# Two token tiles of gMLP's v in place of two gate tiles in the last attention blocks, and an eighth pair of gate columns

## The chip, the cores and the metric

The kernel runs on one core of one Trainium2 chip. The metric is the device time of one execution in microseconds (us). Five engines work side by side, each on a queue of its own and in the order of that queue: TensorE (PE; its weight loads are shown as PEld), VectorE (DVE), ScalarE (ACT), GpSimd (POOL) and SyncE (SP), which here issues nearly all DMAs.

## The reference

One decoder layer works on 576 tokens, 512 of a prompt and 64 of eight running requests, with a model width of 1024:

```python
h   = x @ w_in          # columns: gMLP u | gMLP v | q | k | attention v | gate_A | gate_B
u   = gelu(h_u);  v = LayerNorm(gelu(h_v))
y_A = u * (tril(W_s) @ v_chunk + b_s)        # inside chunks of 128 tokens
y_B = sliding_window_attention(q, k, v_attn) # 16 heads, 4 key heads, sinks, relative bias
m   = (sigmoid(gate_A) * (y_A @ w_pa) + sigmoid(gate_B) * (y_B @ w_pb)) @ w_o
x   = LN1(alpha * x + m);  x = LN2(alpha * x + (silu(x @ w_gate) * (x @ w_up)) @ w_down)
```

gate_A and gate_B have 1024 columns each, so 16 column tiles of 128. u has eight column tiles. v is computed the other way round, with tokens on the partitions: five token tiles (numbers 0 to 3 of 128 prompt tokens each, number 4 of the 64 sample tokens), in two halves of 512 columns.

## The kernel before

**Precision.** Each f32 operand is split in two: `hi`, a rounded copy that ACT makes (line 117), and `lo`, the rest, which DVE makes (line 118). A product is hi*hi + hi*lo + lo*hi, so three matmuls. The weights come from HBM as units of 128x1024 f32 (512 KB, tiles `raw`, three buffers). A unit's `hi` and `lo` have four buffers each, and are written over when PE has read them.

**A plain column tile** (`fm`, called by `column_tile`) takes 8 chunks of the contraction, 3 matmuls each, on two halves of 288 tokens: 48 matmuls 288 wide. **A pair of column tiles** (`pair`) computes two of them together by a Winograd-like scheme with 7 products in place of 8, each of 4 chunks with 3 matmuls: 84 matmuls 288 wide for two tiles. Its products are named B11, T1, T2, B22, B21, T3 and T4. Their weight sides are made by `weight_group` out of two units: DVE and POOL subtract blocks ("sums", step 3; the tiles `t` and `raw`, line 180), and four splits (`ghi`, `glo`) follow in steps 1, 3, 2 and 4, T2 and T3 being parts of `t`. The input's sides S1, S2 and S4 (`XS1`, `XS2`, `XS4`) are made once by `input_sum` out of a second load of x (`xr`, four chunks, two loads of 288 KB each), and S3 (`X<-s`) by `input_sum3`, which writes over a part of `X` that the last v products still read.

**The stages around the change, in order.** (1) Sixteen attention blocks (4 key heads by 4 token blocks). Block i turns its probabilities (`pT`), selects with POOL's masks (`pc`, `pt`), and multiplies by the values (`po`); between these PE runs a fill, which the list `FILLS` names. The last two fills were the gate tiles g0 and g1 (`psg`). ACT's exponentials for the sample tokens (`samS`, line 703) run beside block 14's fill. (2) The first half of v (`acc_v0`): four weight units, and for each of them all five token tiles; the sample's attention values (`pso`) and three of the four `input_sum`s lie in it. (3) The second half of v (`acc_v1`): tiles 0, 1 and 2 one after the other, then 3 and 4 together, with gelu on ACT, and statistics and normalisation (lines 337 to 355, the reciprocal root on POOL as `lnr`) on DVE. (4) The pairs of gates (`merge`, tiles `xg`, `yg`, `zg`), seven of them, where the weights of pair i+1 are prepared beside pair i. A pair's last product, T4, runs inside the next pair. Two `spatial_gate`s (`sgu`) lie in each of pairs 2 to 5, and the key outputs (`pskout`) in pair 1. (5) The output side (`pspa`, `xp`, `acc_o`, `ffn`, `xf`, `d`), which the change does not touch.

Up to stage 3 a scheduler places the instructions of each engine from priorities and its own costs; `issue_after` holds an instruction behind another one. Inside `manual_schedule` (the pairs) the written order counts. SP's queue is one line too: a load of `xr` that waits for its buffer holds the weight loads behind it.

Of the kernel before, what the change touches and what calls it, by code (L numbers as in the profile page):

```python
# [70 lines left out]
FILLS = [tuple(x) for x in "q3 u0 k1 q4 q5 u1 q6 q7 u2 u3 u4 u5 u6 u7 g0 g1".split()]  # L71
# [8 lines left out]
class Builder:  # L80
# [678 lines left out]
    def projections_and_attention(self):  # L759
# [6 lines left out]
        self.kt, self.qs, self.u, self.T = [], {}, [], []  # L766
# [25 lines left out]
        for i, (g, n) in enumerate(blocks):  # L792
# [18 lines left out]
            fill = self.column_tile(*fills[i], ahead=1 + before_last)  # L811
# [18 lines left out]

    def column_tile(self, kind, c, ahead=1):

        ps = self.PS(f"ps{kind}{c}")
        u = self.unit(KC, ahead=ahead)
        self.fm(ps, u, self.xact, ks=range(7))
        yield
        self.fm(ps, u, self.xact, ks=range(7, KC))
        yield
        if kind == "k":
            self.evac_k(ps, c)  # L840
        elif kind == "q":
            self.evac_q(ps, c)
        else:
            tiles = self.u if kind == "u" else self.T
            if c % 2 == 0:
                tiles.append(self.C([2, NT], F32, f"{kind}{c}"))
            self.copied = self.nc.scalar.copy(
                out=tiles[c // 2][:, c % 2].rearrange("p (b c) -> p b c", b=2), in_=ps[:, :, :HB])
# [27 lines left out]
    def gmlp(self):  # L876
# [26 lines left out]
        def tile(t, out, u, ks):  # L903
            for k in ks:
                wh, wl = u[k // 2]
                self.tm(out, (*self.xact(k), self.XS[:, k, :]), wh[:, k % 2], wl[:, k % 2], t, k == 0, k == KC - 1)

        def evacuate(t, acc, half):
# [3 lines left out]
            else:  # L912
# [4 lines left out]
                nc.scalar.activation(out=v[t][:NS, s], in_=low[:NS, :512], func=AF.Gelu_apprx_tanh)  # L917
# [4 lines left out]
        acc = self.accumulators("v0")  # L922
        for n in range(4):
            with self.tc.issue_after(self.copied.ins):
                u = {n: self.unit(2)}
            for t in range(NB + 1):
                tile(t, acc[t], u, (2 * n, 2 * n + 1))
            if n == 0:
                self.sample_rest()
            if n == 1:  # L930
                self.input_sums()
                for c in range(3):
                    self.input_sum(c)
                fourth = self.input_loads(3)
        for t in range(NB + 1):
            evacuate(t, acc[t], 0)
        with self.tc.issue_after(self.turned.ins):
            for t in self.u:
                nc.scalar.activation(out=t[:], in_=t[:], func=AF.Gelu_apprx_tanh)
        us = [self.unit(2, ahead=int(n < 3)) for n in range(4)]  # L940
        for t in range(3):
            acc = self.bank(f"acc_v1_{t}")
            tile(t, acc, us, range(KC))
            if t == 0:
                with self.tc.issue_after(self.last_split.ins):
                    self.input_sum(3, fourth)
# [72 lines left out]
    def merge(self):  # L1019
        nc = self.nc  # L1020
        for t in self.T:
            nc.scalar.activation(out=t[:], in_=t[:], func=AF.Sigmoid)
        left = self.left(self.X, (*self.XSums[:2], self.input_sum3(), self.XSums[2]))
        self.first_pair(self.low_added)
        T = [self.T[0][:, i] for i in range(2)]
        gB = []
# [7 lines left out]
        def gates(i, g, u, more):  # L1034
            def final(x):
                self.copied = nc.scalar.activation(out=g[:, HB:], in_=x, func=AF.Sigmoid)
                nc.scalar.activation(out=u[:], in_=u[:], func=AF.Sigmoid)

            first = lambda: nc.scalar.activation(out=g[:, :HB], in_=g[:, :HB], func=AF.Sigmoid)
            self.pair(f"g{i}", left, g, u, first, final, more)  # L1040
# [370 lines left out]
def _weights(w_in, w_pa, w_pb, w_o, w_gate, w_up, w_down):  # L1411
# [113 lines left out]
```

## Time and profile before

| | |
|---|---|
| runs | median 876.85 us (876.51, 876.85, 876.95) |
| the profiled execution | 876.51 us, its span 874.8 us |
| granted TensorE clock | 0.998 |
| instructions | 14728 |

The page gives each engine's busy time and the chain of work that ended last, which is followed back from the last instruction. The timeline of an engine has the start, the duration, the engine, the line, the operation, output and input and, in brackets, the idle time before it and what ended it. Where several instructions are merged, x2 stands behind them, and the time runs from the first start to the last end. Matmul durations overlap, so a matmul's pace is read from the distance of starts, or from rows of the chain, which don't overlap.

### The profile page before, as it was taken

How to read it: one execution, taken by the hardware profiler on the slowest of the kernel's cores; microseconds unless marked ns; L12 is line 12 of the kernel's file. 1: busy time of each engine (PE TensorE's matmuls, PEld its weight loads, DVE VectorE, ACT ScalarE, POOL GpSimd, SP SyncE). 2: the span in 40 equal slices, each digit the busy share in tenths (PEclk: the TensorE clock that was granted, in tenths of full speed). 3: DMA queues.
4: the chain of work that ended last, by engine and by line, in shares of the span. 5: the costliest groups of instructions: out<-in, count | busy, mean ns of one | idle time of the engine just before them, and what ended most of it. 6: DMA issues, size and time to landing. Idle time of an engine off the chain costs nothing.

```text
span 874.8 us, 14728 instructions
## 1 busy us (share of the span) xinstructions
PE 864.8 (99%) x5907; PEld 816.8 (93%) x5907; DVE 629.4 (72%) x933; ACT 405.5 (46%) x770; POOL 194.5 (22%) x206
## 2 busy tenths in 40 slices
PE   9999999999999999999999999999999999999996
PEld 7999999988899999999888999999999998888885
DVE  5878897657898888767778767777777789124237
ACT  6566566575464464333423544444444557111110
POOL 2013324253242203133203122222222210000003
PEclk9999999999999999999999999999999999999999
DMA  8422124255123134324640032222222335222202
GB/s 304 156 100 62 61 73 148 61 175 163 47 100 102 63 121 142 118 98 157 217 144 0 13 101 91 92 93 91 90 90 95 95 105 188 94 75 95 73 1 108
DMA packets 31168, 91.85 MB, mean 105 GB/s; under 512 B 3963, under 2 KB 9244, under 8 KB 31068
## 3 DMA queue, kind: packets, MB, share of 16 engines
q1 hardware_dynamic: 30764, 88.64, 30.9%
q10 hardware_dynamic: 336, 2.28, 0.7%
q8 instruction: 46, 0.75, 0.4%
q14 instruction: 22, 0.18, 0.1%
HBM read 86.77 MB, written 6.10 MB: 106 GB/s over the span
## 4 chain that ended last, share of the span: by engine, by line
PE 94%; DVE 3%; ACT 1%; DMA 0%; issue 0%; POOL 0%; DVEq 0%; SPq 0%; POOLq 0%; ACTq 0%
PE d L300 16%; PE xf L300 15%; PE zf L300 7%; PE acc_v L300 6%; PE acc_o L300 6%; PE pspa L300 6%; PE xg L300 5%; PE psu L300 5%; PE yf L300 4%; PE psq L300 4%; PE ffn L300 3%; PE xp L300 3%; PE zg L300 3%; PE psav L300 2%; PE psg L300 1%; PE zp L300 1%
## 5 line engine op out<-in xcount | busy, mean ns | idle before, releaser
L118 DVE TENSOR_TENSOR lo<-raw,hi 128x1024 fp32r<-128x1024 f32 x70 | 87.5, 1255 | 94.0 <-ACT hi L117 93.7
L118 DVE TENSOR_TENSOR glo<-raw,ghi 128x1024 fp32r<-128x1024 f32 (+1 forms) x93 | 100.5, 1087 | 53.6 <-ACT ghi L117 53.6
L300 PE MATMUL d<-hi,h 128*128 128x512 f32 (+1 forms) x440 | 128.0, 368 | 0.0
L117 ACT CAST hi<-raw 128x1024 fp32r<-128x1024 f32 x70 | 72.7, 1049 | 103.2 <-PE d L300 82.6
L117 ACT CAST ghi<-raw 128x1024 fp32r<-128x1024 f32 (+1 forms) x93 | 83.4, 900 | 58.7 <-DVE raw L180 56.9
L300 PEld LDWEIGHTS d<-hi,h 128*128 128x128 f32 x440 | 79.9, 189 | 13.8
L300 PE MATMUL d<-lo,h 128*128 128x512 f32 (+1 forms) x242 | 89.6, 370 | 0.0
L180 POOL TENSOR_TENSOR raw<-raw,t 128x512 f32<-128x512 f32 x31 | 41.0, 1323 | 193.3 <-DVE glo L118 164.1
L180 POOL TENSOR_TENSOR t<-raw,raw 128x512 f32<-128x512 f32 x31 | 43.0, 1387 | 111.9 <-DVE raw L180 111.9
L300 PE MATMUL xf<-x1T,ghi 128*128 128x288 f32 x320 | 64.9, 295 | 0.0
L118 DVE TENSOR_TENSOR glo<-t,ghi 128x1024 fp32r<-128x1024 f32 x31 | 63.0, 2032 | 1.9 <-ACT ghi L117 1.9
L300 PEld LDWEIGHTS d<-lo,h 128*128 128x128 f32 x242 | 45.6, 189 | 7.8
L300 PEld LDWEIGHTS xf<-x1T,ghi 128*128 128x128 f32 x320 | 51.3, 188 | 0.3 <-DVE u L231 0.2
L330 POOL TENSOR_SCALAR lnr<-lnmv 128x1 f32<-128x1 f32 (+1 forms) x15 | 12.3, 818 | 169.8 <-DVE lnmv L348 166.5
L645 POOL TENSOR_SCALAR_AFFINE_SELECT pc<-pt 128x512 fp32r<-128x512 f32 x24 | 23.1, 963 | 110.8 <-ACT pt L117 102.7
L300 PE MATMUL xf<-x1T,glo 128*128 128x288 f32 x160 | 47.1, 294 | 0.0
L300 PE MATMUL acc_o<-hi,m 128*128 128x512 f32 x144 | 46.4, 391 | 0.0
L621 ACT ACTIVATE work<-work,att 128x128 f32<-128x128 f32 x64 | 25.0, 392 | 42.1 <-DVE att L618 37.5
L300 PE MATMUL pspa<-yA,hi 128*128 128x288 f32 x256 | 44.3, 294 | 0.0
L300 PE MATMUL psu<-X,hi 128*128 128x288 f32 x256 | 44.1, 294 | 0.0
L300 PE MATMUL acc_v<-hi,X 128*128 128x512 f32 x128 | 41.8, 391 | 0.0
L300 PE MATMUL psq<-X,hi 128*128 128x288 f32 x224 | 38.8, 294 | 0.3 <-DVE kt L513 0.3
(370 smaller groups left out, 2472.6 us busy)
## 6 DMA issues: line engine op xcount, KB each, us to landing
raw<-in_wall_dram SPq DMA_DIRECT2D x132, 512.0 KB
open<-in_open_dram SPq DMA_DIRECT2D x7, 416.0 KB
xr<-in_xT_dram SPq DMA_DIRECT2D x8, 288.0 KB
z<-in_xtok_dram SPq DMA_DIRECT2D x4, 512.0 KB
out_y_prompt_dram<-z SPq DMA_DIRECT2D x3, 512.0 KB
circ<-bout SPq DMA_DIRECT2D x1, 1024.0 KB
Bsel<-circ SPq DMA_DIRECT2D x2, 512.0 KB
kc<-in_kcT_dram SPq DMA_DIRECT2D x2, 512.0 KB
```

Source lines behind the costliest of these rows:

```text
L117: self.nc.scalar.copy(out=hi, in_=src)
L118: return self.nc.vector.tensor_tensor(out=lo, in0=src, in1=hi.bitcast(F32), op=ALU.subtract)
L180: sub = lambda e, out, x, y: e.tensor_tensor(out=out, in0=x, in1=y, op=ALU.subtract)
L300: self.last_mm = self.nc.tensor.matmul(out, l, r, start=start, stop=stop, **more)
L330: self.nc.gpsimd.tensor_scalar_add(r[:n], mv[:n, 1:2], EPS)
L621: nc.scalar.activation(out=pr[:, r], in_=sel[:, r], func=AF.Exp, bias=nm[:, r : r + 1], accum_out=rs[:, r : r + 1])
L645: self.selected = nc.gpsimd.affine_select(out=f(out[:, i]), in_=f(pt[:, i].bitcast(F32)), pattern=[[0, 4], [sign, P]], compare_op=cmp, fil ...
```

## The change

- `FILLS` ends with v0 and v1 in place of g0 and g1. The new `value_tile` computes token tiles 0 and 1 of v's first half there, and ACT copies the sums to `v0raw`; gelu and statistics follow after the attention. For these tiles all four weight units of v's first half are converted before the attention ends.
- The first half of v then has only tiles 2, 3 and 4. Its unit buffers are kept for it, and each unit of the second half is converted (`ahead=0`) when tiles 2 to 4 have used a unit of the first. The sample's values move behind the second unit, the `input_sum`s to one per unit, and the gelus of u behind tile 4's first gelu.
- g0 and g1 become pair 0 of eight. The gates' first sigmoid moves from the middle of a pair to its end, and `first_pair`, the first pair's weight split, is written ahead of `input_sum3`.

```diff
-FILLS = [tuple(x) for x in "q3 u0 k1 q4 q5 u1 q6 q7 u2 u3 u4 u5 u6 u7 g0 g1".split()]
+FILLS = [tuple(x) for x in "q3 u0 k1 q4 q5 u1 q6 q7 u2 u3 u4 u5 u6 u7 v0 v1".split()]
...
+    def value_tile(self, t):
+        ps = self.PS(f"psv{t}")
+        if t == 0:
+            self.v0w = [self.unit(2, ahead=int(n < 3)) for n in range(4)]
+            self.v0raw = self.C([2, 512], F32, "v0raw")
+        self.value_part(t, ps[:, 0], self.v0w, range(7))
+        yield
+        self.value_part(t, ps[:, 0], self.v0w, range(7, KC))
+        yield
+        self.copied = self.nc.scalar.copy(out=self.v0raw[:, t], in_=ps[:, 0])
...
-        acc = self.accumulators("v0")
+        acc = {t: self.bank(f"acc_v0_{t}") for t in (2, 3, NB)}
+        with self.tc.issue_after(self.turned.ins):
+            for t in range(2):
+                evacuate(t, self.v0raw[:, t], 0)
+        us = []
         for n in range(4):
-            with self.tc.issue_after(self.copied.ins):
-                u = {n: self.unit(2)}
-            for t in range(NB + 1):
-                tile(t, acc[t], u, (2 * n, 2 * n + 1))
+            for t in acc:
+                tile(t, acc[t], self.v0w, (2 * n, 2 * n + 1))
+            us.append(self.unit(2, ahead=0))
             if n == 0:
-                self.sample_rest()
-            if n == 1:
                 self.input_sums()
-                for c in range(3):
-                    self.input_sum(c)
-                fourth = self.input_loads(3)
+                chunk = self.input_loads(0)
+            else:
+                if n == 1:
+                    self.sample_rest()
+                self.input_sum(n - 1, chunk)
+                chunk = self.input_loads(n)
...
-        with self.tc.issue_after(self.turned.ins):
+        with self.tc.issue_after(self.gelu.ins):
             for t in self.u:
                 nc.scalar.activation(out=t[:], in_=t[:], func=AF.Gelu_apprx_tanh)
-        us = [self.unit(2, ahead=int(n < 3)) for n in range(4)]
...
-        for t in self.T:
-            nc.scalar.activation(out=t[:], in_=t[:], func=AF.Sigmoid)
+        self.first_pair(self.low_added)
         left = self.left(self.X, (*self.XSums[:2], self.input_sum3(), self.XSums[2]))
-        self.first_pair(self.low_added)
...
-                nc.scalar.activation(out=u[:], in_=u[:], func=AF.Sigmoid)
-
-            first = lambda: nc.scalar.activation(out=g[:, :HB], in_=g[:, :HB], func=AF.Sigmoid)
-            self.pair(f"g{i}", left, g, u, first, final, more)
+                for t in (g[:, :HB], u[:]):
+                    nc.scalar.activation(out=t, in_=t, func=AF.Sigmoid)
+
+            self.pair(f"g{i}", left, g, u, lambda: None, final, more)
...
-            for i in range(7):
+            for i in range(8):
```

Of the program's order, three places follow. Names carry a running number, which differs between the two programs.

**ACT at the end of the attention**, from the last exponential of the last block (line 623) on; `pt_2` and `pt_3` are the last two blocks' turned probabilities, `bot` the lower half of their values. Before:

```order
L623 ACTIVATE att<-att 128x4
L847 COPY u_2094<-psu_2096 128x576
L117 CAST pt_2_2157<-pT_2_2152 128x512
L658 COPY bot_1_2170<-po_1_2165 64x512
L703 ACTIVATE samS,satt<-samS,satt 128x136 x8
L705 ACTIVATE satt<-satt,misc 128x8
L117 CAST pt_3_2292<-pT_3_2287 128x512
L658 COPY bot_2_2305<-po_2_2300 64x512
L847 COPY g_2309<-psg_2226 128x576
L658 COPY bot_3_2359<-po_3_2354 64x512
L847 COPY g_2309<-psg_2311 128x576
```

Of the change:

```order
L623 ACTIVATE att<-att 128x4
L117 CAST hi_2241<-raw_2227 128x1024
L867 COPY u_2094<-psu_2096 128x576
L117 CAST pt_2_2157<-pT_2_2152 128x512
L658 COPY bot_1_2170<-po_1_2165 64x512
L703 ACTIVATE samS,satt<-samS,satt 128x136 x8
L705 ACTIVATE satt<-satt,misc 128x8
L117 CAST pt_3_2275<-pT_3_2270 128x512
L658 COPY bot_2_2288<-po_2_2283 64x512
L850 COPY v0raw<-psv_2226 128x512
L658 COPY bot_3_2320<-po_3_2315 64x512
L850 COPY v0raw<-psv_2293 128x512
```

One weight cast, that of v's fourth unit, has come ahead of block 14's turned probabilities; on DVE its `lo` stands at the same place. The copies of the fills are those of v instead of g.

**DVE ahead of the first pair of gates**, from the statistics of v's tile 2 on; `glo_0` is the low part of B11 and T1, `glo_2` of T3 and T2, `glo_4` of B22 and B21, `X<-s` are the four chunks of S3, `vlow` is tile 4's sum. Before:

```order
L337 BN_STATS lnst<-v_2416 128x6
L348 BN_AGGR lnmv<-lnst 128x2
L118 TENSOR_TENSOR X<-s_0_2553,X 128x288
L353 SCALAR_TENSOR_TENSOR v_2416<-v_2416,lnmv,lnvg 128x1024
L118 TENSOR_TENSOR X<-s_0_2553,X 128x288
L355 SCALAR_TENSOR_TENSOR v_2416<-v_2416,lnr,lnvb 128x1024
L118 TENSOR_TENSOR X<-s_1_2554,X 128x288 x2
L118 TENSOR_TENSOR glo_0_2886<-raw_2699,ghi_0_2885 128x1024
L118 TENSOR_TENSOR glo_2_2892<-t_2881,ghi_2_2891 128x1024
L915 TENSOR_TENSOR vlow_2863<-acc_v_4_2822,vlow_2863 64x512
L118 TENSOR_TENSOR glo_4_2896<-raw_2705,ghi_4_2895 128x1024
```

Of the change:

```order
L337 BN_STATS lnst<-v_2374 128x6
L348 BN_AGGR lnmv<-lnst 128x2
L118 TENSOR_TENSOR X<-s_0_2415,X 128x288
L353 SCALAR_TENSOR_TENSOR v_2374<-v_2374,lnmv,lnvg 128x1024
L118 TENSOR_TENSOR X<-s_0_2415,X 128x288
L355 SCALAR_TENSOR_TENSOR v_2374<-v_2374,lnr,lnvb 128x1024
L118 TENSOR_TENSOR glo_0_2767<-raw_2529,ghi_0_2766 128x1024
L118 TENSOR_TENSOR X<-s_1_2416,X 128x288
L118 TENSOR_TENSOR glo_2_2773<-t_2762,ghi_2_2772 128x1024
L118 TENSOR_TENSOR X<-s_1_2416,X 128x288
L930 TENSOR_TENSOR vlow_2753<-acc_v_4_2712,vlow_2753 64x512
L118 TENSOR_TENSOR glo_4_2777<-raw_2565,ghi_4_2776 128x1024
```

Two of S3's four chunks now stand behind `glo_0`. Further ahead on DVE, the last chunk of the input's sums stands between the two halves of tile 0's normalisation, as the scheduler put it, and on ACT the four gelus of u stand between tile 4's first gelu and tile 2's second.

**ACT from the end of pair 0 into pair 1** (pair 0's tile is `T_2902` before and `T_2791` now, pair 1's `T_3021` and `T_2909`; `ghi_2`, `ghi_4`, `ghi_0`, `ghi_6` are the splits for pair 1's B22 and B21, its T2 and T3, pair 2's B11 and T1, and pair 1's T4). Before:

```order
L252 COPY T_2902<-xg_2903 128x288
L1039 ACT_TABLE_LOAD
L1039 ACTIVATE T_2902<-T_2902 128x288
L117 CAST ghi_2_2999<-raw_2906 128x1024
L117 CAST ghi_4_3017<-t_2908 128x1024
L243 COPY T_3021<-xg_3022 128x288
L246 COPY T_3021<-zg_3024 128x288
L117 CAST ghi_0_3056<-raw_2950 128x1024
L1036 ACTIVATE T_2902<-xg_2903 128x288
L1037 ACTIVATE T_2902<-T_2902 128x576
L117 CAST ghi_6_3076<-raw_2906 128x512
L252 COPY T_3021<-xg_3022 128x288
```

Of the change:

```order
L252 COPY T_2791<-xg_2792 128x288
L117 CAST ghi_2_2887<-raw_2795 128x1024
L117 CAST ghi_4_2905<-t_2797 128x1024
L243 COPY T_2909<-xg_2910 128x288
L246 COPY T_2909<-zg_2912 128x288
L117 CAST ghi_0_2944<-raw_2839 128x1024
L1052 ACT_TABLE_LOAD
L1052 ACTIVATE T_2791<-xg_2792 128x288
L1054 ACTIVATE T_2791<-T_2791 128x288
L1054 ACTIVATE T_2791<-T_2791 128x576
L117 CAST ghi_6_2965<-raw_2795 128x512
L252 COPY T_2909<-xg_2910 128x288
```

The first sigmoid and the load of the sigmoid's table have left the place ahead of `ghi_2`, and stand ahead of `ghi_6`.

More of the change, by code (lines that the diff above doesn't have):

```diff
@@ L810, in projections_and_attention @@
             before_last = i + 2 == len(blocks)
-            fill = self.column_tile(*fills[i], ahead=1 + before_last)
+            if fills[i][0] == "v":
+                fill = self.value_tile(fills[i][1])
+            else:
+                fill = self.column_tile(*fills[i], ahead=1 + before_last)
             next(fill, None)
@@ L843, in column_tile @@
         else:
-            tiles = self.u if kind == "u" else self.T
             if c % 2 == 0:
-                tiles.append(self.C([2, NT], F32, f"{kind}{c}"))
-            self.copied = self.nc.scalar.copy(
-                out=tiles[c // 2][:, c % 2].rearrange("p (b c) -> p b c", b=2), in_=ps[:, :, :HB])
+                self.u.append(self.C([2, NT], F32, f"{kind}{c}"))
+            self.nc.scalar.copy(
+                out=self.u[c // 2][:, c % 2].rearrange("p (b c) -> p b c", b=2), in_=ps[:, :, :HB])
     def small_tables(self):
@@ L916, in evacuate @@
                     out=low[:NS, :512], in0=acc[:NS], in1=low[:NS, :512], op=ALU.add)
-                nc.scalar.activation(out=v[t][:NS, s], in_=low[:NS, :512], func=AF.Gelu_apprx_tanh)
+                self.gelu = nc.scalar.activation(out=v[t][:NS, s], in_=low[:NS, :512], func=AF.Gelu_apprx_tanh)
             if half == 0 or t < 3:
@@ L945, in gmlp @@
                 with self.tc.issue_after(self.last_split.ins):
-                    self.input_sum(3, fourth)
+                    self.input_sum(3, chunk)
             evacuate(t, acc, 1)
@@ L1020, in merge @@
         nc = self.nc
[L1021 to L1022 removed]
+        self.first_pair(self.low_added)
         left = self.left(self.X, (*self.XSums[:2], self.input_sum3(), self.XSums[2]))
[L1024 to L1026 removed]
+        T, gB = [], []
         yA, yB = [], []
@@ L1053, in merge @@
                     g, u = t[:, 0], t[:, 1]
-                (T if i < 3 else gB).extend((g, u))
-                if i == 6:
+                (T if i < 4 else gB).extend((g, u))
+                if i == 7:
                     self.spots = (0, 4, 5, 6)
-                gates(i, g, u, i < 6)
+                gates(i, g, u, i < 7)
         for w in self.todo:
@@ L1433, in _weights @@
     fm(col(o_q, 2))
-    start = {"q": o_q, "k": o_k, "u": 0, "g": o_g}
+    start = {"q": o_q, "k": o_k, "u": 0}
     for kind, c in FILLS:
-        fm(col(start[kind], c))
+        if kind != "v":
+            fm(col(start[kind], c))
     for i in range(2):
         tm(w_in[:, o_v + 512 * i : o_v + 512 * i + 512])
-    for j in range(2, 16, 2):
+    for j in range(0, 16, 2):
         pair(col(o_g, j), col(o_g, j + 1))
```

16 lines of the change are left out of this document (9 added, 7 removed).

## The prediction

> **What bounds the kernel now.** I read the page's busy times first, then its chain of work that ended last, by engine.
>
> ```profile
> PE 864.8 (99%) x5907; PEld 816.8 (93%) x5907; DVE 629.4 (72%) x933; ACT 405.5 (46%) x770; POOL 194.5 (22%) x206
> ...
> PE 94%; DVE 3%; ACT 1%; DMA 0%; issue 0%; POOL 0%; DVEq 0%; SPq 0%; POOLq 0%; ACTq 0%
> ```
>
> PE carries 94% of the chain, so a matmul that goes is gained in full, unless something that PE waits for comes later. Next is that chain in order of time, from the last fills to the second pair of gates (start, duration, what).
>
> ```profile
> 168.91 6.53 PE psg L300 x48
> ...
> 176.81 5.47 PE psg L300 x42
> 182.28 0.91 PE po L300 x4
> 183.18 0.80 PE psg L300 x6
> ...
> 184.01 0.65 ACT g L847
> ...
> 194.87 44.67 PE acc_v L300 x196
> 239.54 1.58 PE xg L300 x12
> ...
> 247.49 3.18 PE xg L300 x24
> ...
> 258.65 0.11 PE pskout L581
> ...
> 259.08 2.92 PE xg L300 x22
> ```
>
> PE has one wait of 0.65 us here, for ACT's copy of g1. Third, what the helpers have left from v's start to the pairs (windows: length, PE, PEld, DVE, ACT and POOL busy, clock), cut where v's second half begins: that half has 112 matmuls at 44.67/196 = 0.228 us, so 25.5 us, and 239.54 - 25.5 = 214.04. I call this moment T0.
>
> ```profile
> 185.49:214.04 28.55, 28.55 (x185) 23.26 (x185) 18.88 (x33) 22.41 (x37) 12.07 (x9) 1.00 0.59 192
> 214.04:239.54 25.50, 25.50 (x115) 21.14 (x114) 21.62 (x30) 10.16 (x17) 7.76 (x7) 1.00 0.11 32
> ```
>
> The clock is 1.00, PE is never idle, and DVE works 18.88 + 21.62 = 40.50 of 54.05 us. How closely DVE runs ahead of PE shows at three low parts that PE uses soon after they are written: pair 0's B11, and T2 of pairs 1 and 2 (timelines of PE and DVE).
>
> ```profile
> 239.63 0.29 PE L300 MATMUL xg<-X,glo 128*128 128x288 f32 x1
> ...
> 253.97 0.29 PE L300 MATMUL xg<-XS2h,glo 128*128 128x288 f32 x1
> ...
> 265.57 0.29 PE L300 MATMUL xg<-XS2h,glo 128*128 128x288 f32 x1
> ...
> 231.32 0.68 DVE L337 BATCH_NORM_STATS2 lnst<-v 128x6 f32<-128x512 f32 x1
> ...
> 236.17 1.22 DVE L118 TENSOR_TENSOR glo<-raw,ghi 128x1024 fp32r<-128x1024 f32 x1
> ...
> 239.57 0.68 DVE L915 TENSOR_TENSOR vlow<-acc_v,vlow 64x512 f32<-64x512 f32 x1 [1.04 <-ACT vlow L914]
> ...
> 247.53 0.46 DVE L231 TENSOR_TENSOR T<-yg,T 128x288 f32<-128x288 f32 x1 [0.34 <-PE yg L300]
> ...
> 249.44 1.23 DVE L118 TENSOR_TENSOR glo<-raw,ghi 128x1024 fp32r<-128x1024 f32 x1 [0.26 <-ACT ghi L117]
> ...
> 250.95 2.17 DVE L118 TENSOR_TENSOR glo<-t,ghi 128x1024 fp32r<-128x1024 f32 x1
> ...
> 261.20 1.23 DVE L118 TENSOR_TENSOR glo<-raw,ghi 128x1024 fp32r<-128x1024 f32 x1 [0.79 <-ACT ghi L117]
> ...
> 262.71 2.23 DVE L118 TENSOR_TENSOR glo<-t,ghi 128x1024 fp32r<-128x1024 f32 x1
> ```
>
> Pair 0's part is ready at 237.39 and used at 239.63, a slack of 2.24 us. Pair 1's is ready at 253.12 and used at 253.97: 0.85. Pair 2's is ready at 264.94 and used at 265.57: 0.63. So PE is the bound, but by less than a microsecond, and DVE is next.
>
> **The change, part by part.** *Matmuls.* g0 and g1 go: 6.53 + 5.47 + 0.80 = 12.80 us. An eighth pair comes: from 247.49 (pair 0's T3) to 259.08 (pair 1's T3) a pair takes 11.59, of which four `pskout` are 0.43, so 11.16. The 48 matmuls of v's tiles 0 and 1 take 48 x 0.228 = 10.94 wherever they stand. The first g tile took 6.53, the second 6.27; the 0.26 between them lies in the switch from the small matmuls ahead and may stay. The saving is 12.80 - 11.16 = 1.64 at most, 1.38 at least; I take 1.5.
>
> *Shorter fills, one split more.* Block 14's fill falls from 6.53 to 24 x 0.228 + 0.2 = 5.67, the first part of block 15's from 5.47 to 21 x 0.228 = 4.79, so PE reaches the last `po` at 182.28 - 0.86 - 0.68 = 180.74. It needs POOL's last selection there, at the end of this row of ACT, DVE and POOL:
>
> ```profile
> 166.45 0.64 ACT L847 COPY u<-psu 128x576 f32<-128x576 f32 x1 [0.41 <-PE psu L300]
> ...
> 175.97 0.59 ACT L117 CAST pt<-pT 128x512 fp32r<-128x512 f32 x1 [0.23 <-PE pT L635]
> ...
> 167.62 0.69 DVE L118 TENSOR_TENSOR pt<-pT,pt 128x512 fp32r<-128x512 f32 x1 [0.44 <-ACT pt L117]
> ...
> 179.66 1.22 POOL L645 TENSOR_SCALAR_AFFINE_SELECT pt<-pt 128x512 fp32r<-128x512 f32 x2
> ...
> 207.66 1.05 ACT L117 CAST hi<-raw 128x1024 fp32r<-128x1024 f32 x1 [0.41 <-PE acc_v L300]
> ...
> 208.74 1.22 DVE L118 TENSOR_TENSOR lo<-raw,hi 128x1024 fp32r<-128x1024 f32 x1 [1.00 <-ACT hi L117]
> ```
>
> v's fourth unit overwrites u7's, so its cast starts when u7's fill ends, 166.45, and its low part ends at 166.45 + 1.05 + 1.22 = 168.72, where `pt`'s started at 167.62: 1.1 later. The sample's scores and exponentials behind it on DVE and ACT slip as much, and the cast of the last `pt`, which had 0.23 to spare, by 0.8. POOL ends at 179.66 + 1.22 + 0.8 = 181.7. The last of `po`'s four matmuls comes at 180.74 + 3/4 of 0.91 = 181.4, so PE waits 0.3; it had 1.4 before, so bounds are 0 and 1.0, and I take 0.2 since DVE's ops overlap a little. ACT's copy ahead of the sample's turn stays (0.65 then, a little less for 512 columns).
>
> *DVE up to the pairs.* Here the change takes 10.94 us of PE's cover away, and of DVE's work only three low parts (3 x 1.22 = 3.66, made inside the attention): 36.84 in 43.1 us. The places where it must wait matter now. I follow the chain from T0 in the new order, with these rows and those above (SP issues a chunk of x; POOL starts when it has landed; POOL's root; gelu of u).
>
> ```profile
> 207.22 0.33 SPq L976 DMA_DIRECT2D xr<-in_xT_dram  x1
> ...
> 211.13 0.80 POOL L980 TENSOR_TENSOR s<-xr 128x288 f32<-128x288 f32 x1 [5.67 <-DMA xr<-in_xT_dram]
> ...
> 225.28 0.57 POOL L331 TENSOR_TENSOR lnr<-lnr,mhalf 128x1 f32<-128x1 f32 x1
> ...
> 192.56 1.16 ACT L939 ACTIVATE u<-u 128x1152 f32<-128x1152 f32 x1
> ```
>
> The last unit can be cast only at T0, when its buffer is free: 1.05 + 1.22, behind which come two 0.4 us low parts of chunk 2, so SP can issue the last chunk's loads at about T0 + 4.8. They land 211.13 - 207.22 = 3.9 later (T0 + 8.7); POOL does S3's difference (0.8), tile 0's root (0.57 and an estimated 0.3 for the op ahead of it) and the chunk's sum (0.8): T0 + 11.2. DVE needs four ops of 0.4, half a normalisation (1.2) and tile 4's sum (0.6): T0 + 14.5. ACT's gelu of tile 4 (0.6), the four gelus of u (about 4.5) and tile 2's (0.6) stand in one line: T0 + 20.2. From that gelu to the end of `glo_0` DVE took 237.39 - 231.32 = 6.07 before; two chunks of S3 (0.8) now stand behind it: 5.3, so T0 + 25.5. Before it was 237.39 - 214.04 = T0 + 23.35. DVE has slipped by 2.1 against PE, and pair 0's slack of 2.24 just holds. T0 + 25.5 is a price worked out from rows in new places; with POOL's three steps (0.8, 0.87 and 0.8) at twice their length it is 2.4 more, and where three of DVE's four ops of 0.4 lie beside POOL's, 1.2 go.
>
> *At pair 1's T2* the slip grows by the two chunks of S3 (0.8) and shrinks by waits of DVE that are filled up now (1.04 + 0.34 + 0.26 = 1.64): 2.1 + 0.8 - 1.64 = 1.26, less the slack of 0.85, so PE stalls 0.4. *At pair 2's* DVE also gains the wait of 0.79 at `ghi`, since no first sigmoid stands ahead of it any more, but loses about 0.95: pair 0's table load and a third sigmoid now stand ahead of `ghi_6`.
>
> ```profile
> 245.59 1.28 ACT L1039 ACT_TABLE_LOAD   x1
> 248.02 0.44 ACT L1039 ACTIVATE T<-T 128x288 f32<-128x288 f32 x1 [1.14 <-DVE T L231]
> ```
>
> Slip 1.42, less 0.63: stalls of 0.8 in all by then. From pair 2's T3 on the spatial gates, four matmuls and one each, lengthen PE's pairs and DVE catches up. So this term is +0.8, with bounds 0 (1.2 off) and 3.2 (2.4 on).
>
> A rule speaks against the change here. The load above takes 1.28, and where nothing else holds ACT the next activation follows at once. The Trainium skill, ScalarE: Activation LUTs, section What ACT_TABLE_LOAD costs, adds a drain of about 1.38 us to such a load, some 2.66 in all. By it the moved load would cost pair 2 another 1.38 and the sum below would be 877.4; by the row it is 876.0. The trace can't exclude a drain at this place, since ACT waited for DVE behind the load anyway.
>
> *Edits at nothing.* The gates' sigmoids and the `v0raw` copies lie on ACT, at 46%, beside matmuls; without cover a third sigmoid would cost 0.44 a pair. The weight stream stays at three `raw` buffers. From pair 3 on each pair is as before.
>
> **Sum.** 876.51 (the profiled execution; its span is 874.8, and 1.7 lies around it) - 1.5 + 0.2 + 0.8 = 876.0. The median of the runs is 0.34 above the profiled one.
>
> **Rivals.** (a) *DVE keeps pace.* If the chain from T0 takes 0.8 less, for instance because the last chunk lands at T0 + 8, no stall is left: 876.51 - 1.5 = 875.0, or 875.2 with the attention's wait. For it speaks that DVE's small ops can lie beside POOL's; against it, that the slacks were 0.85 and 0.63. (b) *The DVE chain becomes the bound*, slower than before: with POOL's steps at twice their length the stall is 3.2, 876.51 - 1.3 + 3.2 = 878.4. From a stall of 1.3 the change loses, from 3.1 on measurably so. DVE's 36.84 in 43.1 us speaks for it, the idle 6 us against. (c) *The attention's cover breaks*: POOL's last selection at +1.0 instead of +0.2, 876.8. (d) *The table load with the drain*: 877.4. (e) *More is gained than matmuls*: fewer table loads or filled waits, beyond 1.75 us; no row shows PE waiting for those, so 875 or less only with luck.
>
> **How the numbers follow.** A difference of 0.2%, 1.75 us, is about what a measurement of this kernel can tell from none. Chances: the forecast 0.47, (a) 0.25, (b) 0.15, (c) 0.05, (d) 0.03, (e) 0.05. Faster by over 0.2% means under 875.1: (e) and a third of (a), 0.12. Slower by over 0.2% means over 878.6: most of (b) and a bit of (d), 0.15. The rest, 0.73, is within. The range holds all of (a) and (c) and the nearer half of (b): 874.9 to 878.6. The forecast's own is 875.3 to 877.5.
>
> **What would show it.** In the trace of the changed kernel: 12 fewer 288-wide matmuls; `acc_v` starting about 1.4 us earlier (near 184.1) and pair 0 about 12.4 earlier (near 227.1); PE waiting for a `glo` on DVE at T2 of pairs 1 and 2, and not in pairs 3 to 7; DVE waiting for POOL's sum of the last chunk between tile 0's two normalisation steps; two table loads after the attention instead of four. The prediction is wrong if PE waits in v itself for a low part, if pair 0's first low part comes over 1 us after PE asks for it, or if PE never waits in the pairs.

## The result, and the profile after

The changed kernel is slower by about a microsecond: 878.20 us in the median of 21 runs (877.60 to 880.52) against 877.13 of the kernel before (876.51 to 878.28), a ratio of 1.0014 with a 95% interval of 1.0007 to 1.0020. That is 1.07 us more, within the 0.2% of the forecast, but on the other side of zero. The profiled executions say the same: 877.79 against 876.51, spans of 876.1 and 874.8.

The busy times and the chain of work that ended last, in the page of the changed kernel:

```profile
PE 864.6 (99%) x5895; PEld 815.3 (93%) x5895; DVE 630.3 (72%) x940; ACT 406.4 (46%) x775; POOL 192.8 (22%) x208
...
PE 71%; DVE 3%; ACT 2%; DMA 1%; issue 1%; POOL 1%; DVEq 0%; POOLq 0%; SPq 0%; ACTq 0%
```

There are 12 matmuls fewer, as forecast, and PE's share of the chain falls from 94% to 71%. That does not mean that 23% of the time is lost: the chain leaves PE at each place where PE waited and follows the others back from there. The places are what counts, and the waits of PE from pair 0 to the end of the gates are few (what waits, for what, us in total, times, longest):

```profile
PE xg L300 <- ACT T L252: 0.7, 1, 0.7
PE xg L300 <- DVE T L231: 0.5, 1, 0.5
```

The view counts only part of each: the distance of two matmul starts, less the usual distance at that place (0.13 inside a product), gives more, and is used below. The chain in order of time (start, duration, what), in the piece ahead of the first of these waits:

```profile
238.79 1.14 DVE glo L118
...
240.30 1.09 DVE glo L118
...
243.80 1.05 ACT ghi L117
...
244.87 1.28 ACT L1052
...
246.17 0.41 ACT T L1052
246.58 0.90 ACT T L1054 x2
247.48 0.24 ACT ghi L117
...
247.89 0.41 ACT T L252
...
248.34 3.45 PE xg L300 x24
```

L1052 is the sigmoid of `final`, here with its table load; L1054 are the two other sigmoids; L252 is the copy of `x` to `u` ahead of T3, which adds into the same bank. PE's timeline on both sides, first now, then before:

```profile
247.39 0.27 PE L582 MATMUL pskout<-ident,misc 128*64 128x128 f32 x1
248.34 0.54 PE L300 MATMUL xg<-X,ghi 128*128 128x288 f32 x2 [0.68 <-ACT T L252]
```

```profile
258.81 0.27 PE L582 MATMUL pskout<-ident,misc 128*64 128x128 f32 x1
258.84 0.51 PE L300 MATMUL xg<-X,ghi 128*128 128x288 f32 x2
```

So pair 1's T3 comes 0.95 after the transpose ahead of it, where before it came 0.03 after: 0.92 later (the expectations below put it at 0.98). The second wait is at the very end of the gates, at the last pair's T4:

```profile
326.68 0.56 PE L300 MATMUL pspa<-yA,hi 128*128 128x288 f32 x3
327.75 0.53 PE L300 MATMUL xg<-X,ghi 128*128 128x288 f32 x2 [0.52 <-DVE T L231]
```

The third of those `pspa` matmuls starts at 326.94, and T4 at 327.75: 0.68 lost, for DVE's addition of T3, which ends at 327.70.

To see where the time went, I cut each trace at the starts of the same matmuls. The cut begins with the first `po`, because the first loads of a program land at times of their own: `po` begins at 55.57 in the trace of before and at 55.89 to 58.74 in the others, where nothing ahead of it was changed.

| us | first `po` to v | v | first pair to end of `pspa` | from there to the last matmul | sum |
|---|---|---|---|---|---|
| before | 129.68 | 54.13 | 170.07 | 458.06 | 811.94 |
| changed | 128.38 | 43.26 | 183.23 | 458.04 | 812.91 |
| difference | -1.30 | -10.87 | +13.16 | -0.02 | +0.97 |

The length of a pair is taken here from the first matmul of its T1 (of its B11 in pair 0) to that of the next pair's T1. An undisturbed pair without spatial gates takes 11.15 (pair 6 does), so of the 13.16 there are 2.01 of waits: 0.32 in pair 0 (11.46 long), 1.04 in pair 1 (12.64 against 11.60 before), none in pairs 2 to 6 (13.38 for each of pairs 2 to 5, with their spatial gates, as before), and the rest, 0.65, at the end.

### The profile page after: what moved, and what is told of

Same layout as the page of the kernel before. It is cut to its first block, busy times and chain, and to the rows that moved or that the text cites. A ratio compares the mean times of both kernels' runs of the same rounds, so it can differ in the third digit from the quotient of the medians.

```text
span 876.1 us, 14722 instructions
## 1 busy us (share of the span) xinstructions
PE 864.6 (99%) x5895; PEld 815.3 (93%) x5895; DVE 630.3 (72%) x940; ACT 406.4 (46%) x775; POOL 192.8 (22%) x208
## 4 chain that ended last, share of the span: by engine, by line
PE 71%; DVE 3%; ACT 2%; DMA 1%; issue 1%; POOL 1%; DVEq 0%; POOLq 0%; SPq 0%; ACTq 0%
PE d L300 16%; PE xf L300 15%; PE zf L300 7%; PE acc_o L300 6%; PE pspa L300 6%; PE xg L300 4%; PE yf L300 4%; PE ffn L300 3%; PE xp L300 3%; PE zg L300 2%; PE zp L300 1%; PE acc_v L300 1%; PE sgu L300 1%; PE yg L300 1%; DVE glo L118 1%
## 5 line engine op out<-in xcount | busy, mean ns | idle before, releaser
L118 DVE TENSOR_TENSOR lo<-raw,hi 128x1024 fp32r<-128x1024 f32 x68 | 85.1, 1255 | 95.6 <-ACT hi L117 95.3
L118 DVE TENSOR_TENSOR glo<-raw,ghi 128x1024 fp32r<-128x1024 f32 (+1 forms) x96 | 104.0, 1086 | 53.9 <-ACT ghi L117 53.9
L117 ACT CAST ghi<-raw 128x1024 fp32r<-128x1024 f32 (+1 forms) x96 | 86.1, 900 | 72.7 <-DVE raw L180 59.9
L117 ACT CAST hi<-raw 128x1024 fp32r<-128x1024 f32 x68 | 70.8, 1048 | 105.7 <-PE d L300 82.6
L180 POOL TENSOR_TENSOR raw<-raw,t 128x512 f32<-128x512 f32 x32 | 43.3, 1352 | 199.5 <-DVE glo L118 169.4
L330 POOL TENSOR_SCALAR lnr<-lnmv 128x1 f32<-128x1 f32 (+1 forms) x15 | 11.2, 746 | 168.1 <-DVE lnmv L348 164.7
L300 PE MATMUL xg<-X,ghi 128*128 128x288 f32 x192 | 39.8, 299 | 1.2 <-ACT T L252 0.7
L117 ACT CAST ghi<-t 128x1024 fp32r<-128x1024 f32 x32 | 33.5, 1047 | 13.4 <-PE xg L300 7.8
```

Of the source, the lines that this page charges most:

```text
L117: self.nc.scalar.copy(out=hi, in_=src)
L118: return self.nc.vector.tensor_tensor(out=lo, in0=src, in1=hi.bitcast(F32), op=ALU.subtract)
L180: sub = lambda e, out, x, y: e.tensor_tensor(out=out, in0=x, in1=y, op=ALU.subtract)
L300: self.last_mm = self.nc.tensor.matmul(out, l, r, start=start, stop=stop, **more)
L330: self.nc.gpsimd.tensor_scalar_add(r[:n], mv[:n, 1:2], EPS)
```

## The experiments

Each kernel differs from the one named by the diff shown. "Sum" is the column above, read from the trace; the ratio is that of the runs to runs of the kernel before on the same chip.

**The table load alone, at an earlier place** (from the changed kernel):

```diff
         nc.scalar.copy(out=u[:, hi], in_=z)
+        if name == "g0":
+            nc.scalar.activation(out=u[:, 0:1], in_=g[:, 0:1], func=AF.Sigmoid)
         do(2)
```

> The changed kernel with one edit: a sigmoid of a single column behind pair 0's copy of T1, in a place where ACT stood idle for 2.48 us, so that the table load is done there and not ahead of pair 0's final sigmoid. In the changed kernel PE stands 0.98 us (247.39 to 248.34) at pair 1's T3, for ACT's copy of u, and ahead of that copy ACT had the load (1.28), three sigmoids and a cast. Theory A (the load on ACT's line is the wait): the load's 1.28 is more than the 0.98, so the wait is gone; about 877.2 (1.0 under the changed kernel), no change on any other engine. Theory B (DVE is behind, ACT's cast of 243.80 waits for DVE's difference, and the load only fills that wait): at least 0.6 of the wait stays; 877.8 to 878.2.

Measured: 877.00 us against 876.99, ratio 1.0002 (0.9993 to 1.0011); sum 811.98, so 0.93 less than the changed kernel. ACT's timeline at both places:

```profile
231.10 0.40 ACT L246 COPY T<-zg 128x288 f32<-128x288 f32 x1
231.52 1.28 ACT L248 ACT_TABLE_LOAD   x1
...
244.04 1.05 ACT L117 CAST ghi<-raw 128x1024 fp32r<-128x1024 f32 x1 [2.62 <-DVE raw L180]
245.00 0.41 ACT L1054 ACTIVATE T<-xg 128x288 f32<-128x288 f32 x1
```

The load lies in a gap, the sigmoid follows the cast at once, and the wait at T3 is gone. DVE's rows are where they were (ACT's cast still waits 2.62 us for DVE's difference). Theory A holds: DVE's lateness does not make this wait without the load.

**PE's order alone at the end of the gates** (from the changed kernel):

```diff
-        self.end_pairs()
         for g in range(len(yA), 8):
             part(yA, self.u[g // 2][:, g % 2], self.C, f"yA{g}")
+        u0, ps0 = self.unit(KC, ahead=1), [self.bank(f"pspa0_{b}") for b in range(2)]
+        self.fm(ps0, u0, lambda k: (yA[k][:, 0], yA[k][:, 1]), ks=range(4))
+        with self.tc.issue_after(self.last_mm.ins):
+            self.end_pairs()
+        self.fm(ps0, u0, lambda k: (yA[k][:, 0], yA[k][:, 1]), ks=range(4, KC))
```

> The changed kernel with PE's order alone moved at the end of the gates: the last pair's T4 behind 24 matmuls of the first pspa product; it was behind 9 in the changed kernel, and behind 21 before the change. In the changed kernel PE stands 0.68 us at that T4 (327.07 to 327.75) for DVE's addition of T3, which ends at 327.70. Theory A (the order written by the scheduler put too little between T3 and T4): 24 matmuls take 3.2 us, the addition is done 1.4 us earlier than T4, the wait is gone; about 877.5 (0.7 under the changed kernel). Theory B (DVE and ACT are late there by the third sigmoid and the parts of yA, and pspa's own parts are as late): PE waits as long for a part of yA or the unit's low part inside those 24; 878.2.

Measured: 877.36 us, ratio 1.0000 (0.9992 to 1.0009); sum 812.05, 0.86 less. PE and DVE there:

```profile
329.16 0.43 PE L300 MATMUL pspa<-yA,lo 128*128 128x288 f32 x2
329.43 0.42 PE L300 MATMUL xg<-X,ghi 128*128 128x288 f32 x2
```

```profile
326.49 1.22 DVE L118 TENSOR_TENSOR lo<-raw,hi 128x1024 fp32r<-128x1024 f32 x1
327.62 0.45 DVE L231 TENSOR_TENSOR T<-xg,T 128x288 f32<-128x288 f32 x1
```

T4 follows without a gap. DVE's addition is no earlier against PE than in the changed kernel; only what PE does meanwhile differs. Theory A.

**The same edit in the kernel before**, a control:

> The kernel before with the edit of t4_behind_24 alone: the last pair's T4 behind 24 matmuls of pspa and not 21. PE had no wait there (0.10 us at the switch). Theory A (the edit only mends what the changed kernel's order broke): 877.0, the same as before. Theory B (the edit is a gain in any kernel, so early_and_t4 owes its lead to it): 876.4.

Measured: 878.82 us, ratio 1.0018 (1.0009 to 1.0027); sum 813.27, 1.33 more than before. Both theories missed. The same lines did not put T4 behind 24 matmuls here: in the trace it stands behind 38 (T3's last matmul starts at 328.33, T4 at 333.62). And PE waits at the first `xp` pair, where on DVE six of the parts SA and SB stand ahead of the next stage's weight parts, and four did before:

```profile
361.83 0.43 PE L300 MATMUL xp<-Y,ghi 128*128 128x288 f32 x2
363.26 0.40 PE L300 MATMUL xp<-Y,glo 128*128 128x288 f32 x1 [1.00 <-DVE glo L118]
```

So this run is no control for 24 matmuls in the kernel before, and what made the wait at `xp` was not followed: the changed kernel has six of these parts ahead as well, without such a wait. What the edit could have won there is small all the same: PE's switch to the last T4 was 0.10 longer than usual in the trace of before. The order ahead of T4 has to be read again in each kernel.

**The sigmoids put back, in the changed kernel, and moved alone, in the kernel before:**

```diff
 # sigmoid_mid_pair, from the changed kernel (before_end_sigmoid: the reverse edit in the kernel before)
-                for t in (g[:, :HB], u[:]):
-                    nc.scalar.activation(out=t, in_=t, func=AF.Sigmoid)
-            self.pair(f"g{i}", left, g, u, lambda: None, final, more)
+                nc.scalar.activation(out=u[:], in_=u[:], func=AF.Sigmoid)
+            first = lambda: nc.scalar.activation(out=g[:, :HB], in_=g[:, :HB], func=AF.Sigmoid)
+            self.pair(f"g{i}", left, g, u, first, final, more)
```

> The changed kernel with the first sigmoid of each pair back behind B21's addition, as before the change; nothing else is edited. The table load then stands in pair 0 ahead of the casts for pair 1's B22, T3 and T2; T4 of the last pair then stands behind 18 matmuls of pspa and not 9. Theory A (the load and the third sigmoid on ACT's line make the two waits of 0.98 and 0.68): both go, but the low part of pair 1's T2, which came with 0.06 us to spare (242.39 against 242.45), comes up to 1.1 later (1.28 + 0.44 less 0.58 that ACT stood idle), so PE waits 0.9 to 1.1 there: 877.3 to 877.7. Theory B (the end-of-pair place is no worse than the old one, DVE alone is late): waits of 2 us in all stay and a part of 1 is added: 878.5 to 879.2.

> The kernel before with the sigmoids' edit alone (first sigmoid of a gate pair at its end, beside the other two). DVE is not late here at pair 0. The last pair's T4 then stands behind 13 matmuls of pspa and not 21. Theory A (the sigmoids' edit costs something also without the shorter cover): at pair 1's T3 nothing (DVE's 2.1 us slip is missing, so ACT's line starts that much earlier), at the last T4 the addition of T3 ends at 327.88 on the trace of before, T3 ends at 325.2, 13 matmuls take 1.7: a wait of 0.7 to 1.0, so 877.13 + 0.9 = 878.0. Theory B (only together with the slip of DVE): same as before, 877.1.

Measured: put back 878.09 us, ratio 1.0009 (1.0000 to 1.0017), sum 812.77; moved alone 877.09, ratio 0.9999 (0.9991 to 1.0008), sum 811.96, the same as before. Theory A's number for the first (877.3 to 877.7) missed. T3's wait went as it said, but waits of 0.25 at pair 0's T4, 0.21 at pair 1's T2 and 0.26 at pair 2's T2 came in its place, and the last T4 waits longer, though it stands behind 18 matmuls, since DVE's addition now stands behind a low part that waits for ACT:

```profile
327.72 0.43 PE L300 MATMUL pspa<-yA,lo 128*128 128x288 f32 x2
328.88 0.40 PE L300 MATMUL xg<-X,ghi 128*128 128x288 f32 x1 [0.72 <-DVE T L231]
```

In the kernel before, where the first parts of pair 0 come in good time, the same edit costs nothing measurable. There too it puts the load and the third sigmoid ahead of pair 1's copy of `u`, which then ends at 259.31, and T3 starts at 259.50 without a wait:

```profile
258.91 0.40 ACT L252 COPY T<-xg 128x288 f32<-128x288 f32 x1
```

Before, the copy was 1.57 early; here it is 0.19 early. The edit has used up the slack and not more. Its expectation of 0.7 to 1.0 at the last T4 missed too: the addition of T3 ends there 1.78 us after T3's last matmul starts (2.81 before, behind other parts of yA), and 13 matmuls just cover that. In these runs the sigmoids' edit does harm only where ACT is already late.

**The first weight split back behind S3** (from the changed kernel):

```diff
-        self.first_pair(self.low_added)
         left = self.left(self.X, (*self.XSums[:2], self.input_sum3(), self.XSums[2]))
+        self.first_pair(self.low_added)
```

> The changed kernel with the first weight split back behind the input's S3, as before the change; DVE then makes all four low parts of S3 ahead of the first low part of pair 0, where now two stand ahead of it. That part was ready at 227.44, and PE used it at about 227.65; the load of the weights for pair 1 is issued when it is done (227.44) and took 4.42 us. Theory A (DVE's line ahead of pair 0 is what is late): the part comes 0.8 later, PE waits 0.6 at pair 0's B11, and what hangs on the weights for pair 1 comes 0.8 later too, against a PE that is 0.6 later: 878.2 + 0.6 to 0.8 = 878.8 to 879.0. Theory B (this part of the change does nothing, ACT's load alone is late): 878.2.

Measured: 878.71 us, ratio 1.0019 (1.0010 to 1.0029); sum 813.50, 0.59 more. DVE and PE (the two low parts of S3 that had stood behind stand ahead of `glo`, which ends at 228.26):

```profile
226.30 0.82 DVE L118 TENSOR_TENSOR X<-s,X 128x288 fp32r<-128x288 f32 x2
227.04 1.22 DVE L118 TENSOR_TENSOR glo<-raw,ghi 128x1024 fp32r<-128x1024 f32 x1
...
227.62 0.42 PE L300 MATMUL xg<-X,ghi 128*128 128x288 f32 x2
228.32 0.40 PE L300 MATMUL xg<-X,glo 128*128 128x288 f32 x1 [0.27 <-DVE glo L118]
```

DVE's line ahead of pair 0 has little slack left (0.34 in the changed kernel, where the part ends at 227.44 for a matmul at 227.78), as the prediction's chain said, and this part of the change was worth 0.6.

**u's gelus as early as before** (from the changed kernel):

```diff
-        with self.tc.issue_after(self.gelu.ins):
+        with self.tc.issue_after(self.turned.ins):
             for t in self.u:
```

> The changed kernel with the four gelus of u allowed as soon as the attention's last tile is turned, as before the change; they then lie among the copies of the sample's attention, and not (4.32 us) between the gelu of v's last rows and that of tile 2. DVE stood idle 0.77 and 0.35 us there. Theory A (DVE's line is late by what it waits for here): pair 0's first low part comes up to 1.1 earlier, the weights for pair 1 too, DVE's difference and with it ACT's line at pair 1's T3 start 1.1 earlier, and the wait of 0.98 is gone or 0.2: 877.2 to 877.5. Theory B (the chain to that part goes through POOL's sums and the last chunk's loads, which the gelus don't touch, or the early gelus hold up ACT's casts as long): under 0.3 gained, 877.9 to 878.2.

Measured: 877.64 us, ratio 1.0009 (1.0000 to 1.0018); sum 812.23, 0.68 less, between the theories. Pair 0's first low part came 0.6 earlier and not 1.1, pair 0 had no wait at all (11.14), and T3's wait at pair 1 fell from 0.92 to 0.71:

```profile
247.30 0.27 PE L582 MATMUL pskout<-ident,misc 128*64 128x128 f32 x1
...
248.04 0.40 PE L300 MATMUL xg<-X,ghi 128*128 128x288 f32 x1 [0.47 <-ACT T L252]
```

Why 0.6 and not 1.1 shows on DVE. Its wait of 0.35 for the late gelu is gone, but of the wait of 0.77 ahead of it 0.47 stays, and that one is for POOL's reciprocal root, which the gelus don't touch. First the changed kernel, then this run:

```profile
220.45 1.28 DVE L355 SCALAR_TENSOR_TENSOR v<-v,lnr,lnvb 128x1024 f32<-128x1024 f32 x1 [0.77 <-POOL lnr L331]
...
220.60 1.28 DVE L355 SCALAR_TENSOR_TENSOR v<-v,lnr,lnvb 128x1024 f32<-128x1024 f32 x1 [0.47 <-POOL lnr L331]
```

**DVE relieved in pair 0** (from the changed kernel), by two empty steps ahead of the list of work between the products:

```diff
+        self.todo = [lambda: None] * 2 + self.todo
         self.todo += [lambda g=g: part(yA, ...
```

> The changed kernel with the list of work between the products (v's last normalisations, the spatial gates, the parts of yA) begun one pair later; DVE then has 4 us less to do in pair 0 and the last pair has a gate in it again, T4 stands behind 13 matmuls of pspa and not 9. Theory A (at pair 1's T3 the load and DVE's late difference add up, so relief of DVE takes that wait away as well as the early load did; at the end DVE has 1.8 us of gate work more and 13 matmuls take 0.5 more than 9): T3's wait of 0.98 gone, the last wait 0.7 to 1.5, so 877.3 to 878.0. Theory B (ACT's line alone makes T3's wait, DVE only seems late): T3's wait stays, 878.2 or more.

Measured: 877.25 us, ratio 1.0000 (0.9991 to 1.0009); sum 812.18. That is just under theory A's range, but not for its reasons. T3's wait stayed at 0.90. DVE, with less to do, waits for the weights, so that ACT's cast comes only 0.48 earlier against the start of pair 1 (4.34 after it in place of 4.82):

```profile
239.16 2.23 DVE L118 TENSOR_TENSOR glo<-t,ghi 128x1024 fp32r<-128x1024 f32 x1
242.02 0.69 DVE L180 TENSOR_TENSOR t<-raw,raw 128x512 f32<-128x512 f32 x1 [0.63 <-DMA raw<-in_wall_dram]
```

And the edit does more than was meant: the key outputs (`pskout`) stand in the same list and moved to pair 2, so PE, too, comes to T3 earlier, by their 0.45. The run therefore does not tell the two theories apart at T3. The last T4, on the other hand, found its addition just done: it ended 1.78 us after T3's last matmul started, and 13 matmuls in between make 1.85. In the changed kernel it ended 1.95 after, and 9 make 1.3. So it is the few matmuls that leave T4 waiting, not a slower DVE.

**The edits together.** First the two that took a wait away. Then, on top of them, DVE's sum of v's sample rows ahead of the second low part of pair 0 (the first diff below), or, in its place, u's early gelus. Last, with these gelus, POOL's memset behind the attention's last selection (the second diff).

```diff
-            with self.tc.issue_after(before.ins) if before and x == "3" else nullcontext():
+            with self.tc.issue_after(before.ins) if before and x in "23" else nullcontext():
...
+        with self.tc.issue_after(self.selected.ins):
-        nc.gpsimd.memset(v[NB][NS:], 0.0)
+            nc.gpsimd.memset(v[NB][NS:], 0.0)
```

> The changed kernel with both edits that took a wait away: the table load early in pair 0 and the last pair's T4 behind 24 matmuls of pspa. From the first matmul of the attention's po to the last matmul, the changed kernel took 812.91 us, the kernel before 811.94, the first edit alone 811.98, the second 812.05. Theory A (two waits on PE that have nothing to do with each other): the gains add up, 812.91 - 0.93 - 0.86 = 811.1, which is 0.8 under the kernel before, so about 876.3 or a ratio of 0.999. Theory B (a wait taken away at pair 1 comes back later): 811.9 to 812.0, a ratio of 1.000.

> The kernel of early_and_t4 with one more edit: DVE's addition for the sample rows of v stands ahead of the second low part of pair 0 (for T3 and T2), not behind it. In the changed kernel PE stood 0.31 us at pair 0's T2 (230.57 to 230.90, one matmul being 0.13, and 0.10 behind it), for ACT's copy of B11, which stood behind the gelu of those rows, which waited 1.61 us for that addition. Theory A: the wait goes, 0.3 less than early_and_t4. Theory B (the second low part then comes later than T2 needs it): nothing gained, or a wait on DVE instead at the same place.

> The changed kernel with three edits: the table load early in pair 0, the last pair's T4 behind 24 matmuls of pspa, and u's gelus among the sample's attention. From the first matmul of po to the last matmul, early_and_t4 took 811.36; in u_gelu_early pair 0 took 11.14 us in place of 11.57 and pair 1 had no wait at T2 (0.11). Theory A (each wait is one of its own): 811.36 - 0.43 - 0.11 = 810.8, 1.1 under the kernel before (811.94): about 875.9, a ratio of 0.9987. Theory B (the gelus' gain is the same that the early load already brought): 811.3, a ratio of 0.9993.

> The kernel of all_three with one more edit: POOL's memset of v's unused rows (0.95 us) stands behind the attention's last selection and not between the two parts of it. In the changed kernel POOL did the memset from 178.97, the selections' last part ended at 181.80, and PE, whose fill is 1.5 us shorter, stood 0.24 us at the last po (181.38 to 181.85, a matmul being 0.23). Theory A (the wait hangs on POOL's line): the selections end up to 0.9 earlier, the wait is gone; the stretch from the first po to v's first matmul falls from 128.44 to about 128.2, the rest as in all_three: 0.24 less, about 875.75, which the runs can hardly tell but the trace can. Theory B (the wait hangs on the later cast and low part of the attention's last tile, one split more being ahead of them): POOL waits for that low part instead, and the stretch stays at 128.4.

| | us | before, same chip | ratio (95%) | sum |
|---|---|---|---|---|
| early_and_t4 | 876.41 | 876.98 | 0.9994 (0.9985 to 1.0002) | 811.36 |
| both_and_low_row | 876.34 | 876.98 | 0.9992 (0.9984 to 1.0001) | 811.14 |
| all_three | 875.98 | 877.12 | 0.9987 (0.9978 to 0.9995) | 811.04 |
| all_three_memset_behind | 875.55 | 877.43 | 0.9978 (0.9969 to 0.9987) | 810.56 |

The two large waits are separate: taking away both won 1.55 by the sums, where one by one they had won 0.93 and 0.86; of the missing 0.24, about 0.1 lies in the attention (128.44, against 128.36 and 128.35 with one edit) and 0.1 in pair 0 (11.57, against 11.49 and 11.45). The low row's edit took pair 0's wait at T2 away and left one of 0.29 at its T3. The early gelus won 0.32 on top, between the two expectations, and the memset 0.48, of which 0.34 in the attention, where the selections end 0.85 earlier (181.15 against 182.00) and the wait at the last `po` is gone, as theory A said, and 0.11 in pair 0. The last kernel beats both: 1.4 us less than before by the sums, 2.35 less than the changed kernel. POOL and the page's chain line of it:

```profile
179.33 0.64 POOL L647 TENSOR_SCALAR_AFFINE_SELECT pc<-pt 128x512 fp32r<-128x512 f32 x1 [0.17 <-DVE pt L118]
179.92 1.23 POOL L647 TENSOR_SCALAR_AFFINE_SELECT pt<-pt 128x512 fp32r<-128x512 f32 x2
181.20 0.95 POOL L922 MEMSET v<- 64x1024 f32 x1
```

```profile
PE 94%; DVE 3%; ACT 1%; DMA 1%; issue 0%; POOL 0%; DVEq 0%; SPq 0%; ACTq 0%; POOLq 0%
```

With the waits gone PE carries 94% again, and what the matmuls alone were worth can be read off.

## Why the prediction was wrong

The forecast was 876.0, 0.5 under the profiled execution of before. The measured change of the sum is +0.97. None of the three signs that were to show the prediction wrong appeared: they all watched DVE's low parts, and PE lost its time elsewhere. Step by step:

- **Matmuls, -1.5: right.** With nearly all waits taken away the sum is 1.38 lower, one wait of 0.11 being left.
- **The attention, +0.2: right in size, short of a cause.** PE stood 0.24 at the last `po`, and POOL's selections ended at 181.80 where the working had 181.7. What made them end there was also the memset of 0.95 between them. It had stood there before too, and was not read as something that a shorter fill uncovers.
- **DVE up to the pairs: right.** `glo_0` was to be ready at T0 + 25.5. T0 is 202.02 now, and the part ends at 227.44, so T0 + 25.42. The steps on the way came as said, so this is no luck: POOL's sum of the last chunk at T0 + 11.1 (11.2 forecast), tile 4's sum at T0 + 14.7 (14.5), the gelu of tile 2 at T0 + 20.0 (20.2). Only DVE's busy time in v was off, 32.75 where 36.84 was forecast; of the difference 1.95 is work that has moved behind pair 0's start. The chain did not rest on it. The slip against PE is 1.9 where 2.1 was forecast. The row, and PE's first matmuls of pair 0:

```profile
226.22 1.22 DVE L118 TENSOR_TENSOR glo<-raw,ghi 128x1024 fp32r<-128x1024 f32 x1
...
227.53 0.42 PE L300 MATMUL xg<-X,ghi 128*128 128x288 f32 x2
227.78 0.29 PE L300 MATMUL xg<-X,glo 128*128 128x288 f32 x1
```

- **The waits at T2 of pairs 1 and 2, +0.8: the step that failed.** They measured 0.11 and 0, and in their place PE stood 0.32 in pair 0, 0.92 at pair 1's T3 and 0.65 at the last T4. The low part of pair 1's T2 ended at 242.39 and its matmul started at 242.45, 0.06 later, as T3 started 0.05 after its copy and the last T4 0.05 after its addition: no slack was left, as forecast, but PE had already stood 0.32 in pair 0. At pair 2's T2 the part ended at 253.27 for a matmul at 255.09. DVE did lose its time behind `ghi_6` (0.87, the first row below, for 0.95 forecast), but PE had lost 0.92 at T3 by then. Besides, DVE's part, which had taken 2.23 before, took 1.21 here, and POOL's difference beside it 2.50 in place of 1.29:

```profile
248.02 0.69 DVE L118 TENSOR_TENSOR glo<-raw,ghi 128x512 fp32r<-128x512 f32 x1 [0.87 <-ACT ghi L117]
...
252.06 1.21 DVE L118 TENSOR_TENSOR glo<-t,ghi 128x1024 fp32r<-128x1024 f32 x1
...
251.91 2.50 POOL L180 TENSOR_TENSOR raw<-raw,t 128x512 f32<-128x512 f32 x1 [5.84 <-DVE glo L118]
```

- **The failing sentence** is "pair 0's table load and a third sigmoid now stand ahead of `ghi_6`", priced at 0.95 on DVE's low parts. What else stood behind them on ACT's queue was not followed: `ghi_6` is followed by the copy of `u` (L252), and T3, which adds into the same bank, waits for that copy. The trace of before had the row that prices it, and it was not shown:

```profile
254.53 1.06 ACT L117 CAST ghi<-raw 128x1024 fp32r<-128x1024 f32 x1 [1.83 <-DVE raw L180]
255.49 0.40 ACT L1036 ACTIVATE T<-xg 128x288 f32<-128x288 f32 x1
255.78 0.67 ACT L1037 ACTIVATE T<-T 128x576 f32<-128x576 f32 x1
256.36 0.61 ACT L117 CAST ghi<-raw 128x512 fp32r<-128x512 f32 x1
256.87 0.40 ACT L252 COPY T<-xg 128x288 f32<-128x288 f32 x1
```

The copy ended at 257.27 and T3 started at 258.84: a slack of 1.57. (The chain of the prediction has T3 at 259.08, since it counts from the end of the transpose ahead of it.) Now the way from the cast to the copy's end is 1.75 longer (4.49 against 2.74), and the cast comes 0.80 later against the pair's start, T1's first matmul (4.82 after it, against 4.02). 1.57 - 1.75 - 0.80 = -0.98; T3 itself was due 0.11 later by the wait at T2 and follows the copy by 0.05, which makes the 0.92 that was measured. Of the 1.75 the load is 1.41: from the cast's start to the first sigmoid's start it takes 2.37 with the load and 0.96 without (`table_early`), 1.28 for the load itself and the rest because the instructions on its two sides no longer overlap. The third sigmoid is the other 0.34.

The experiments show that it takes both terms. Without the load there is no wait, though DVE is as late; with the load and the third sigmoid, but DVE not late (`before_end_sigmoid`), there is none either; with DVE 0.6 earlier, of which pair 0's own wait takes half, it is 0.2 less.

- **"From pair 3 on each pair is as before": right for pairs 2 to 6, wrong for the last.** The last pair of before still had a spatial gate's work on DVE in it, pair 7 has none, and the scheduler put 9 matmuls of `pspa` between its T3 and T4 in place of 21; that the one led to the other is not shown. I had read PE's order at the front of the gates only. That is 0.65 of the 0.97.
- **"Edits at nothing".** The sigmoids cost nothing in the kernel before, as said; behind a late DVE they, with the load, cost a wait.
- **Pair 0's T2, not foreseen.** 0.31, since ACT's copy of B11 stood behind a gelu that waited for DVE's sum of the sample rows.
- **The rivals.** (a) did not come: DVE slipped as in the forecast. (b) gave 878.4, which is near the result, but by DVE's chain alone, and that stall of 3.2 did not come; the nearness is luck. (c) was 0.24 and not 1.0. (e) did not show: the gates and v now need two table loads fewer, and with nearly all waits gone the gain is still no more than that of the matmuls. (d) put the table load at the right place on ACT with the wrong price, a drain behind it. The load began 0.02 after the cast ahead of it and the sigmoid 0.02 after its end. The Trainium skill, ScalarE: Activation LUTs, section What ACT_TABLE_LOAD costs, gives 2.66 us with a drain; no trace here shows the drain on ACT's line, and the load cost 1.41 on that line, as worked out above.

What stays open: why the scheduler put so few matmuls ahead of the last T4, and why the kernel before waits at `xp` when its T4 is moved.

## What to carry to other kernels

When cover of PE is taken away, list every row behind which PE waits in the stage that follows, on each engine's queue, with its slack in the trace of before: a moved instruction is paid by all that stands behind it in the queue, not by the next row alone. Read the new order also at the far end of the changed stage, where a scheduler may put less work between a result and its use. A one-off cost such as a table load can be put in an idle gap by a tiny operation of the same function, as it was here.

## What the runs showed of the hardware

In pair 1 of the changed kernel a low part of 128x1024 took 2.18 us on DVE (240.21 to 242.39) where the one ahead of it took 1.22; POOL's difference ran from 240.01 to 241.31, and from its end to the end of DVE's is 1.08:

```profile
240.21 2.18 DVE L118 TENSOR_TENSOR glo<-t,ghi 128x1024 fp32r<-128x1024 f32 x1
...
240.01 1.30 POOL L180 TENSOR_TENSOR raw<-raw,t 128x512 f32<-128x512 f32 x1 [0.79 <-DVE glo L118]
```

That is what one engine's waiting for the whole of the other's instruction looks like. In pair 2 it is POOL's difference that takes the longer time (2.50, and 1.21 on DVE, in the rows shown for pair 2's T2 above), though POOL's record starts first in both. The Trainium skill, SBUF — State Buffer, section Who interferes with whom, states such an exclusive lock of DVE and POOL for a DVE instruction with two inputs in SBUF (the on-chip memory), and the rows agree with the lock; which of the two engines gets it can't be read from the recorded starts. It is this blocked part that left pair 1's T2 without slack.
